# Near-attention head loads behind the last value store, reciprocals by two blocks, gates in quarters

## The chip, the cores and the metric

The kernel runs on one core of one Trainium2 chip. The metric is device time in microseconds (us) of one execution. A core has five engines with an instruction queue each: TensorE (PE, matmuls; its weight loads are PEld in the profile), VectorE (DVE), ScalarE (ACT), GpSimd (POOL) and SyncE (SP), which in this kernel issues nearly all DMA transfers. In the traces here an engine takes its instructions in the order of its queue: what waits holds up all that stands behind it.

## What is computed

A two-layer encoder on 1024 tokens of width 1024. The change lies in the second (odd) layer. Cut to that:

```python
qc, kc, vc, qm, gate = split_cols(h @ w_in_odd[o], SPLIT_ODD)
yc = neighborhood_attn(qc, kc, vc, rpb_c[o])      # 16 heads of 64
ym = memory_attn(qm, mk, mv)                      # 4 heads of 128, 256 memory tokens
y = jnp.concatenate([yc, ym], axis=-1) * jax.nn.silu(gate)
x = x + y @ w_out_odd[o]
```

`neighborhood_attn` is softmax attention on the 16 x 64 token grid in which each query sees a clamped window of 8 rows by 16 columns, with a learned bias by offset. The tokens are permuted so that for one block of 128 queries all keys lie in the block itself and its two neighbours. The kernel calls these heads the near heads.

## The kernel before, in words

**Arithmetic.** Every float32 operand of a large product is split into a high and a low part (`h`, `l`), and three products are summed. So each product first needs a copy on ACT and a subtraction on DVE or POOL, also for the transposed probabilities (`p_parts`, L527: `ph` on ACT at L117, then `pl` on DVE).

**Stages of the second layer.** After `front` (input projections, to about 1036 us), `odd` runs the memory attention (to about 1145 us) and then the near heads (`near`, about 1145 to 1393 us); `out_project` follows. While the memory attention runs, a generator `work` fills PE with what is left of the projections: the gate of one tile, the values of the last near heads (`values_of_two`, two calls `a` and `b`), and the first keys. `values_of_two` evicts each 128 tokens into a tile `vt` (ACT copy, DVE subtraction at L414) and stores it to the DRAM tensor `vd` (L415, rows `v<-vt`); there are three `vt` buffers, shared with the gate's. Behind `b` and the first keys, `work` asks for what the first near head needs: two bias tiles (`near_bias`, L1046, rows `bm<-offsets`, 320 KB each) and the values of the first pair of heads (`load_v`, rows `v<-v`, 1024 KB). The queries (`load_q`, rows `q<-qc`, two of 512 KB for a pair of heads) are asked for behind the last memory scores; those of the second pair in `near` at its third block, its values at its sixth.

**Who orders it.** The order on PE is pinned to the order of the program from `odd` on. The other queues are ordered by a scheduler that simulates the program when it is built: an instruction goes where its inputs are ready in that simulation, the earlier in the program the sooner, unless it is inside `tc.issue_after(x)`, which keeps it behind the instruction `x`. A load whose buffer is free is therefore put far ahead of its use. Each DMA also carries one of eight semaphores in turn, and is issued only when the transfer eight places before it has landed.

**The near heads.** `near` runs 16 heads of 8 query blocks, 128 steps `n`. At step `n` PE does, in this order: the transpositions of block column `n-4` (`flips`; they read the normalised probabilities `pn` of the up to three blocks that see these keys, the newest of them block `n-3`, which is transposed last), the scores of block `n`, the value products of column `n-5`, and a piece of the filling work (`fill`, 1930 columns on average). A score block goes through: DVE adds the bias and takes the negated maximum (L1079, into `st[:, 0:1]`), ACT does the exponential with its sum (L1082), DVE the reciprocal of the sum (L1083, 128x1), POOL the normalisation in place (L1084, which also halves). There are seven `pn` buffers.

**Side work.** After each score block one step of a list of jobs is issued behind that block's normalisation: the splitting of weights (L451 and L453 on POOL), and, when a pair of heads is done, `gated_steps` (L459): the output `y` of the pair is multiplied by its gate in two halves of 512 columns on DVE (L465, L467), one half a step, then combined on POOL and stored.

Of the kernel before, what the change touches and what calls it, by code (L numbers as in the profile page):

```python
# [9 lines left out]
F32 = mybir.dt.float32  # L10
F32R = mybir.dt.float32r
I32 = mybir.dt.int32
AF = mybir.ActivationFunctionType
OP = mybir.AluOpType
# [9 lines left out]
NEG = -1e30  # L24
# [7 lines left out]
O_Q, O_K, O_V, O_QM, O_G = 0, 8, 16, 24, 28  # L32
# [15 lines left out]
            c=(("P", "P"), ("P", "P"), ("P", "P"), ("yb", "yb"))),  # L48
       dict(y=(("P", "P", "q", "q", "v"), ("k", "k", "k", "k", "q", "q"), ("H",) * 6, ("H",) * 6, ("P", "P", "q", "q", "v"),
               ("k", "k", "k", "k", "q", "q"), ("H",) * 6),  # L50
            c=(("H", "H"), ("H", "H"), ("mk", "sg"), ("yb", "yb"))))
# [13 lines left out]
class Trunk:  # L65
# [317 lines left out]
    def values_of_two(self, w, vd, tag, bank, out, pieces=1, low=None):  # L383

        nc = self.nc
        n = 8 // pieces
        hs, ls = ([t[:, k:k + 2, :] for t in [self.st(tag, [128, n, 256], F32R) for _ in range(pieces)]
                   for k in range(0, n, 2)] for _ in range(2))
        for k in range(0, KT, 2):
            h, l = hs[k // 2], ls[k // 2]  # L390
            with self.ahead("w"):
                raw = self.wload(w[:, :, k * 128:k * 128 + 256].rearrange("h p n -> p h n"))
                raw = raw.rearrange("p (h k n) -> p k h n", h=2, k=2)
                h4, l4 = (t.rearrange("p k (h n) -> p k h n", h=2) for t in (h, l))
                self.copy(h4, raw)
                (low or nc.gpsimd).tensor_tensor(l4, raw, h4, op=OP.subtract)
        yield
        for b in range(0, 8, 2):
            p = self.ps(bank[b // 2 % len(bank)])
            for e in range(2):  # L400
                t = slice((b + e) * 128, (b + e) * 128 + 128)
                for kt in range(KT):
                    for i, (x, m) in enumerate(((0, hs), (0, ls), (1, hs))):
                        self.last = self.pe.matmul(p[:, 256 * e:256 * e + 256], self.h[x][kt][:, t], m[kt // 2][:, kt % 2, :],  # L404
                                                     start=e + kt + i == 0, stop=kt == KT - 1 and i == 2,
                                                     skip_group_check=True)
                    if kt % 4 == 3 and (e == 0 or kt < KT - 1):
                        yield 3072
            for e in range(2):
                o = self.st(out, [128, 2, 2, 2, 64], F32R)  # L410
                src = p[:, e * 256:(e + 1) * 256].rearrange("p (j h d) -> p j h d", j=2, h=2)
                with self.ahead("evict"):
                    self.copy(o[:, :, :, 0, :], src)
                    self.vec.tensor_tensor(o[:, :, :, 1, :], src, o[:, :, :, 0, :], op=OP.subtract)  # L414
                    nc.sync.dma_start(vd[:, :, b + e, :].rearrange("j p n -> p j n"),  # L415
                                      o.bitcast(F32).rearrange("p j h e d -> p j (h e d)"))
            yield 3072

    def gate(self, w, nt, tag="sg"):
# [39 lines left out]
    def gated_steps(self, sg, y, yd, k):  # L459

        nc = self.nc
        first, second = slice(0, 512), slice(512, T)
        dst = yd[k]
        two = lambda t: t.rearrange("p (a n) -> p a n", a=2)
        nc.vector.tensor_tensor(y[:, second], y[:, second], sg[:, second], op=OP.mult)  # L465
        yield
        nc.vector.tensor_tensor(y[:, first], y[:, first], sg[:, first], op=OP.mult)  # L467
        if k < 6:
            yield
            nc.gpsimd.tensor_tensor(sg[:, first], y[:, first], y[:, second], op=OP.subtract)  # L470
            h, l = sg.bitcast(F32R)[:, second], y.bitcast(F32R)[:, second]
            self.copy(h, y[:, second])
            nc.vector.tensor_tensor(l, y[:, second], h, op=OP.subtract)
            nc.sync.dma_start(dst[:, 0:4:2, :], two(y))
            nc.sync.dma_start(dst[:, 1:4:2, :], two(sg))
            return
        nc.sync.dma_start(dst[:, 0:2, :], two(y))
        nc.sync.dma_start(two(sg), yd[k - 6][:, 0:2, :])
        yield
        yield  # L480
        yield
        nc.gpsimd.tensor_tensor(sg[:, second], y[:, first], sg[:, second], op=OP.subtract)
        yield
        nc.gpsimd.tensor_tensor(sg[:, first], y[:, first], sg[:, first], op=OP.subtract)
        nc.sync.dma_start(dst[:, 2:4, :], two(sg))
        yield
        nc.gpsimd.tensor_tensor(y[:, second], sg[:, second], y[:, second], op=OP.subtract)
        nc.sync.dma_start(dst[:, 4, :], y[:, second])
# [554 lines left out]
    def near_bias(self, h):  # L1043

        bm = self.st("bm", [128, 5, 128])
        self.nc.sync.dma_start(bm, self.io["offsets"][h])  # L1046
        return bm

    def near(self, made, load_q, load_v, gate, yd, fill):
# [3 lines left out]

        nc = self.nc
        pts, parts, acc, pair = {}, {}, {}, {}
        first = (made["q0"], made["k0"], made["v0"])
        bms = deque(made["bm"])

        def span(b):
            return max(0, b - 1), min(8, b + 2)  # L1060

        def scores(n):
            h, b = divmod(n, 8)
            q, ks = pair[h // 2]["q"][h % 2], pair[h // 2]["k"][h % 2]
            kh, kl = ks
            lo, hi = span(b)
            w = (hi - lo) * 128
            s = self.ps("s")
            qb = q[:, b * 128:(b + 1) * 128]
            self.pe.matmul(s[:, :w], qb, kh[:, lo * 128:hi * 128], start=True, stop=False)  # L1070
            self.pe.matmul(s[:, :w], qb, kl[:, lo * 128:hi * 128], start=False, stop=True)
            pt = self.st("pn", [128, 384])
            st = self.tiny()
            k0 = (lo - b + 1) * 128
            o = pt[:, k0:k0 + w]
            bm = bms[0]
            bias = bm[:, 2:5:2, :] if b == 0 else bm[:, 0:3:2, :] if b == 7 else bm[:, 1:4, :]
            with self.ahead("exp"):
                nc.vector.tensor_tensor_reduce(o.rearrange("p (k e) -> p k e", e=128),  # L1079
                                               s[:, :w].rearrange("p (k e) -> p k e", e=128), bias,  # L1080
                                               op0=OP.add, op1=OP.min, scale=-1.0, scalar=-NEG, accum_out=st[:, 0:1])
                nc.scalar.activation(o, o, AF.Exp, bias=st[:, 0:1], scale=-1.0, accum_out=st[:, 2:3])  # L1082
                nc.vector.reciprocal(st[:, 3:4], st[:, 2:3])  # L1083
                normal = nc.gpsimd.tensor_scalar(o, o, st[:, 3:4], 0.5, op0=OP.mult, op1=OP.mult)  # L1084
            pts[n] = pt
            for jobs in (self.jobs, self.later_jobs):
                with self.tc.issue_after(normal.ins):
                    while jobs and next(jobs[0], self) is self:
                        jobs.popleft()
                    if jobs:  # L1090
                        break
# [33 lines left out]
        for n in range(128 + 5):  # L1125
# [4 lines left out]
            if n < 128:  # L1130
                j, at = divmod(n, 16)
                if at == 0:
                    if j == 0:
                        q, k, v = first
                    else:
                        q, k, v = pair.pop("q"), made[f"k{j}"], None
# [16 lines left out]
            if n >= 5:  # L1153
                values(n - 5)
                if (n - 5) % 16 == 15:
                    j = (n - 5) // 16
# [721 lines left out]
    def odd(self, w, kvd, yd, vd, mqd, qd, gd):  # L1878
# [8 lines left out]
        nc, tc = self.nc, self.tc  # L1887
# [5 lines left out]
            return sg  # L1893

        def load_q(j):
            return [self.load("q", qd[O_Q + j][i]) for i in range(2)]

        def load_v(j):
            return self.load("v", vd[j // 2][j % 2], (128, 8, 256)).rearrange("p b (h d) -> p b h d", h=2)
        with self.ahead("first"):  # L1900
            kvm = {0: self.load("k", kvd[0], (128, 4, MEM))}
            load = lambda n: self.load("q", mqd[n // 2][:, :, n % 2 * 512:n % 2 * 512 + 512].rearrange("i p n -> p i n"), (128, 2, 512))
# [1 line left out]
        made, first, begun = {}, [], []  # L1904
# [14 lines left out]
        def work():  # L1919
# [14 lines left out]
            yield from k  # L1934
            made["bm"] = [self.near_bias(i) for i in range(2)]
            made["v0"] = load_v(0)
            todo = [(O_K + 1, keys(1)), (O_K + 2, keys(2)), half(5, 0), (O_K + 3, keys(3)), half(5, 512), (O_K + 4, keys(4)),
                    (O_K + 5, keys(5)), half(6, 0), (O_K + 6, keys(6)), half(6, 512), (O_K + 7, keys(7)),
# [56 lines left out]
        for n in range(8):  # L1995
            h, g = divmod(n, 2)
            if g == 0:
                y = self.st("yb", [128, T])
# [4 lines left out]
            o = self.ps("pv")  # L2003
# [8 lines left out]
        while "open" not in made:  # L2012
            fill(1)
        self.due = 0
        self.near(made, load_q, load_v, gate, yd, lambda n: fill(STEP))
        deque(todo, 0)
        self.pe = nc.tensor
# [101 lines left out]
```

## Time and profile before

| | us |
|---|---|
| median of 3 runs | 1513.12 (1510.55 to 1514.97) |
| profiled execution, its own time | 1518.44 |
| its span (first to last instruction) | 1516.7 |
| PE busy in the span | 1480.2 (98%) |
| DVE, ACT, POOL busy | 1042.7, 840.5, 642.5 |
| memory attention and near heads, from the span's start | 1036 to 1393 |

Every duration below is of the profiled execution; 1.7 us of its time lie outside the span. A row of a timeline reads: start, duration, engine, line, operation, output<-input, shape, count, and in brackets how long the engine sat idle before and what released it. Names of tiles stand without their buffer's number. Line numbers are of the kernel before.

### The profile page before, as it was taken

What the parts mean: (1) busy time and instruction counts of PE and PEld (TensorE: products, weight loads), DVE (VectorE), ACT (ScalarE), POOL (GpSimd) and SP (SyncE); (2) the same over time, 40 slices, a digit from 0 to 9 for tenths busy, and PEclk for the clock granted to TensorE, in tenths of its full rate; (3) what the DMA queues carried; (4) which work ended last, traced back from release to release, by engine and by line L of the source; (5) the groups of instructions that cost most, each with busy time, mean ns of one, the idle gap of its engine ahead of it and who ended that gap; (6) DMA issues with size and microseconds to landing.
All of it is one profiled execution on the core that took longest, in us unless ns stands there. A gap on an engine that the chain in (4) does not pass through costs nothing.

```text
span 1516.7 us, 25292 instructions
## 1 busy us (share of the span) xinstructions
PE 1480.2 (98%) x8377; PEld 1272.6 (84%) x8377; DVE 1042.7 (69%) x2117; ACT 840.5 (55%) x1855; POOL 642.5 (42%) x766
## 2 busy tenths in 40 slices
PE   8999999999999999999999999999999999999997
PEld 8898897888888788887879877888898888888886
DVE  7686776777776667777577676654346777788754
ACT  7643664566656456655444444444346777778443
POOL 1323557746675645553450000002324555654455
PEclk9999999999999999999999999999999999999998
DMA  8956334334343524388653344567755577688833
GB/s 292 290 162 182 95 116 156 113 128 124 128 142 97 176 75 143 99 275 276 193 179 125 121 138 137 160 167 265 273 178 174 178 231 228 211 285 314 294 117 137
DMA packets 173859, 271.90 MB, mean 179 GB/s; under 512 B 15648, under 2 KB 96800, under 8 KB 172704
## 3 DMA queue, kind: packets, MB, share of 16 engines
q1 hardware_dynamic: 173296, 270.20, 55.2%
q8 instruction: 66, 1.08, 0.3%
q14 instruction: 65, 0.53, 0.1%
q10 hardware_dynamic: 432, 0.09, 0.0%
HBM read 174.28 MB, written 83.89 MB: 170 GB/s over the span
## 4 chain that ended last, share of the span: by engine, by line
PE 46%; DVE 4%; DMA 3%; issue 1%; ACT 1%; POOL 1%; SPq 0%; POOLq 0%; DVEq 0%; ACTq 0%
PE pj L62 10%; PE x L1532 6%; PE pj L1285 3%; PE pv L62 3%; PE y L1532 3%; PE sa L1285 3%; PE s L62 3%; PE s L1285 2%; PE tr L62 2%; PE tr L1285 2%; PE pv L1532 2%; PE pv L1285 2%; PE y L404 2%; PE pv L404 2%; DMA v<-vt 1%
## 5 line engine op out<-in xcount | busy, mean ns | idle before, releaser
L117 ACT ACTIVATE ph<-tr 128x512 fp32r<-128x512 f32 (+2 forms) x336 | 180.9, 540 | 123.1 <-PE tr L125 82.3
L527 DVE TENSOR_TENSOR pl<-tr,ph 128x512 fp32r<-128x512 f32 (+2 forms) x336 | 205.5, 614 | 55.2 <-ACT ph L117 54.2
L231 PE MATMUL pj<-H,wh 128*128 128x512 f32 x704 | 235.4, 414 | 0.5 <-DVE vt L302 0.2
L147 POOL TENSOR_SCALAR wh<-wraw 128x512 fp32r<-128x512 f32 x48 | 31.8, 665 | 271.3 <-PE x L1532 236.6
L117 ACT ACTIVATE wh<-wraw 128x384 fp32r<-128x384 f32 (+1 forms) x163 | 89.2, 553 | 102.4 <-PE tr L1285 13.5
L231 PE MATMUL pj<-H,wl 128*128 128x512 f32 x352 | 139.6, 397 | 0.0
L231 PEld LDWEIGHTS pj<-H,wh 128*128 128x128 f32 x704 | 120.6, 190 | 18.8 <-POOL wl L149 0.6
L62 PE MATMUL pj<-H,wh 128*128 128x512 f32 x384 | 121.4, 397 | 0.0
L125 PE MATMUL tr<-ident,P 128*128 128x128 f32 x752 | 117.5, 273 | 3.8 <-POOL P L702 1.3
L1084 POOL TENSOR_SCALAR pn<-pn,st 128x384 f32<-128x384 f32 (+1 forms) x128 | 75.2, 588 | 99.7 <-DVE st L1083 60.8
L1233 POOL TENSOR_TENSOR wl<-wraw,wh 128x384 fp32r<-128x384 f32 x56 | 64.1, 1146 | 114.4 <-ACT wh L117 80.4
L125 PEld LDWEIGHTS tr<-ident,P 128*128 128x128 f32 x752 | 89.1, 140 | 13.9 <-POOL P L702 2.6
L1005 ACT ACTIVATE P<-sa,st 128x1024 f32<-128x1024 f32 x64 | 71.6, 1118 | 45.2 <-DVE st L1004 25.4
L1082 ACT ACTIVATE pn<-pn,st 128x384 f32<-128x384 f32 (+1 forms) x128 | 75.1, 587 | 35.4 <-DVE st L1079 33.0
L1007 POOL TENSOR_SCALAR P<-P,st 128x1024 f32<-128x1024 f32 x64 | 74.3, 1164 | 33.7 <-DVE st L1006 28.9
L1004 DVE TENSOR_REDUCE st<-sa 128x1 f32<-128x1024 f32 x64 | 77.6, 1218 | 14.2 <-PE sa L1000 11.3
L62 PE MATMUL s<-k,q 128*128 128x384 f32 (+1 forms) x352 | 86.4, 341 | 0.0
L149 POOL TENSOR_TENSOR wl<-wraw,wh 128x512 fp32r<-128x512 f32 x52 | 68.2, 1313 | 27.0 <-ACT wh L117 24.1
L231 PEld LDWEIGHTS pj<-H,wl 128*128 128x128 f32 x352 | 66.4, 189 | 15.2
L62 PE MATMUL pj<-H,wl 128*128 128x512 f32 x192 | 75.8, 395 | 0.0
L821 PE MATMUL pj<-ah,H 128*128 128x256 f32 x384 | 72.5, 287 | 1.4 <-DVE H L766 1.3
L62 PEld LDWEIGHTS pj<-H,wh 128*128 128x128 f32 x384 | 66.7, 189 | 5.5
(503 smaller groups left out, 4200.6 us busy)
## 6 DMA issues: line engine op xcount, KB each, us to landing
wraw<-w_o SPq DMA_DIRECT2D x52, 256.0 KB, 3.9
y<-yb SPq DMA_DIRECT2D x24, 512.0 KB, 3.3
wraw<-s SPq DMA_DIRECT2D x64, 192.0 KB, 3.3
wraw<-w_e SPq DMA_DIRECT2D x44, 256.0 KB, 3.3
k<-k SPq DMA_DIRECT2D x42, 256.0 KB, 4.3
s<-bias SPq DMA_DIRECT2D x56, 192.0 KB, 2.0
y<-sg SPq DMA_DIRECT2D x20, 512.0 KB, 3.9
wq<-w_o SPq DMA_DIRECT2D x40, 256.0 KB, 3.6
```

What stands on the lines that cost most here:

```text
L62: return lambda *a, **k: self.tc.keep_in_program_order(getattr(self.engine, name)(*a, **k))
L117: return self.nc.scalar.activation(out, in_, AF.Copy, scale=scale)
L125: self.turned = self.fence = self.pe.transpose(o, i, self.ident)
L231: self.pe.matmul(a[:, :n], s[:, kt % UNIT, :], m, start=(kt == 0 and i == 0), stop=(kt == KT - 1 and i == 2))
L527: self.low = nc.vector.tensor_tensor(pl[:, :n], tr[:, :n], ph[:, :n], op=OP.subtract)
L821: self.last = nc.tensor.matmul(a[:, b * 256:(b + 1) * 256], x[kt][:, t], w, start=(kt + b + i == 0), stop=(kt == KT - 1 and i == 2), skip_ ...
L1004: nc.vector.tensor_reduce(st[:, 0:1], s, axis=AX.X, op=OP.max, negate=True)
L1007: self.normal = nc.gpsimd.tensor_scalar(pt, pt, st[:, 2:3], 0.5, op0=OP.mult, op1=OP.mult)
L1082: nc.scalar.activation(o, o, AF.Exp, bias=st[:, 0:1], scale=-1.0, accum_out=st[:, 2:3])
L1084: normal = nc.gpsimd.tensor_scalar(o, o, st[:, 3:4], 0.5, op0=OP.mult, op1=OP.mult)
L1285: last = nc.tensor.matmul(bank, s[:, k, :], y[3 * u + k][m][:, cols], start=start and u + k + e == 0, stop=u == 1 and k + e == 4, skip_gro ...
L1532: self.last = nc.tensor.matmul(bank, ws[s][:, k, :], b[k][m], start=start and k + i == 0, stop=k == UNIT - 1 and i == 2, skip_group_check= ...
```

## The change

Three edits. First, the last store of values is remembered (`self.stored`), and `near_bias`, `load_q` and `load_v` are issued behind it. Second, the statistics of two successive blocks share one `st` tile; the reciprocal is taken once for both, when the second block's sum is there, and then both are normalised one after the other. `self.normal`, behind which the jobs are issued, is then the last normalisation that there is: for a block with an even number that of the pair before. Third, `gated_steps` multiplies in four quarters of 256 columns, one a step.

```diff
@@ values_of_two
-                    nc.sync.dma_start(vd[:, :, b + e, :].rearrange("j p n -> p j n"),
+                    self.stored = nc.sync.dma_start(vd[:, :, b + e, :].rearrange("j p n -> p j n"),
...
@@ gated_steps
-        nc.vector.tensor_tensor(y[:, second], y[:, second], sg[:, second], op=OP.mult)
-        yield
-        nc.vector.tensor_tensor(y[:, first], y[:, first], sg[:, first], op=OP.mult)
+        for i, c in enumerate(slice(p, p + 256) for p in (512, 768, 0, 256)):
+            nc.vector.tensor_tensor(y[:, c], y[:, c], sg[:, c], op=OP.mult)
+            if i < 3:
+                yield
@@ near_bias
-        self.nc.sync.dma_start(bm, self.io["offsets"][h])
+        with self.tc.issue_after(self.stored.ins):
+            self.nc.sync.dma_start(bm, self.io["offsets"][h])
@@ near, scores(n)
-            st = self.tiny()
+            if not begun:
+                begun.append(self.tiny())
+            st, e = begun[0], n % 2
...
-                nc.scalar.activation(o, o, AF.Exp, bias=st[:, 0:1], scale=-1.0, accum_out=st[:, 2:3])
-                nc.vector.reciprocal(st[:, 3:4], st[:, 2:3])
-                normal = nc.gpsimd.tensor_scalar(o, o, st[:, 3:4], 0.5, op0=OP.mult, op1=OP.mult)
+                nc.scalar.activation(o, o, AF.Exp, bias=st[:, e:e + 1], scale=-1.0, accum_out=st[:, 2 + e:3 + e])
+                begun.append(o)
+                if e:
+                    nc.vector.reciprocal(st[:, 4:6], st[:, 2:4])
+                    for i, p in enumerate(begun[1:]):
+                        self.normal = nc.gpsimd.tensor_scalar(p, p, st[:, 4 + i:5 + i], 0.5, op0=OP.mult, op1=OP.mult)
+                    begun.clear()
             pts[n] = pt
             for jobs in (self.jobs, self.later_jobs):
-                with self.tc.issue_after(normal.ins):
+                with self.tc.issue_after(self.normal.ins):
@@ odd
         def load_q(j):
-            return [self.load("q", qd[O_Q + j][i]) for i in range(2)]
+            with tc.issue_after(self.stored.ins):
+                return [self.load("q", qd[O_Q + j][i]) for i in range(2)]
         def load_v(j):
-            return self.load("v", vd[j // 2][j % 2], (128, 8, 256)).rearrange("p b (h d) -> p b h d", h=2)
+            with tc.issue_after(self.stored.ins):
+                v = self.load("v", vd[j // 2][j % 2], (128, 8, 256))
+            return v.rearrange("p b (h d) -> p b h d", h=2)
```

The build shows what the queues become. In the changed kernel the lines after L415 are higher by a few (L985 is L986, L1079 is L1084, L1083 is L1090, L527 is L528).

On SP, in the second half of the memory attention, before. `v_12663` and `v_12843` are the values of the first two pairs of heads, `y_0` and `y_1` the stores of gated memory heads, the rows with `vt` the stores of values.

```order
L506 DMA y_0_83<-sg_12002 128x2x512
L985 DMA v_12663<-v_103 128x2048
L505 DMA y_0_83<-yb_11728 128x2x512
L985 DMA v_12843<-v_103 128x2048
L415 DMA v_105<-vt_12065 128x2x256
L415 DMA v_105<-vt_12069 128x2x256
L1892 DMA sg_12296<-g_9281 128x1024
L415 DMA v_106<-vt_12177 128x2x256
L985 DMA q_12613<-qc_9288 128x1024
L415 DMA v_106<-vt_12181 128x2x256
```

And in the changed kernel, from the last two stores of values on (the names of the loads are the same):

```order
L415 DMA v_106<-vt_12471 128x2x256
L415 DMA v_106<-vt_12475 128x2x256
L986 DMA q_12613<-qc_9288 128x1024
L986 DMA q_12615<-qc_9288 128x1024
L1048 DMA bm_12659<-offsets 128x640
L1048 DMA bm_12661<-offsets 128x640
L986 DMA v_12663<-v_103 128x2048
L986 DMA q_12780<-qc_9289 128x1024
L986 DMA v_12837<-v_103 128x2048
L986 DMA q_12782<-qc_9289 128x1024
L507 DMA y_2_85<-sg_12552 128x2x512
```

Before, ten stores of values stood behind the first `v` load; now all eight first loads of the near heads stand together behind the last store.

On DVE, where the third pair of heads runs and the second pair's `y` is gated, before. `pn_13641` and `pn_13666` are the probabilities of two successive blocks, 34 and 35; L467 multiplies a half of `y`; `pl` is the low part that PE's value products wait for.

```order
L1079 ISA pn_13641,st_13642<-s_13638,bm_13342 128x384
L1079 ISA st_13642 128x1
L467 TENSOR_TENSOR yb_13291<-yb_13291,mk_13317 128x512
L527 TENSOR_TENSOR pl_13635<-tr_13630,ph_13634 128x384
L1079 ISA pn_13666,st_13667<-s_13663,bm_13342 128x384
```

The same blocks in the changed kernel:

```order
L1084 ISA pn_13609,st_13610<-s_13606,bm_13318 128x384
L1084 ISA st_13610 128x1
L466 TENSOR_TENSOR yb_13269<-yb_13269,mk_13293 128x256 x2
L528 TENSOR_TENSOR pl_13603<-tr_13598,ph_13602 128x384
L1084 ISA pn_13632,st_13610<-s_13629,bm_13318 128x384
```

The half has become two quarters in direct succession, at the same place ahead of `pl`. Of the 32 quarters 26 stand so, in 13 couples; six stand apart.

On DVE in the twelfth head, blocks 90, 91 and 92 before (`pn_15209`, `pn_15231`, `pn_15253`, with the reciprocals of their `st` tiles):

```order
L1079 ISA pn_15209,st_15210<-s_15206,bm_14897 128x384
L1079 ISA st_15210 128x1
L527 TENSOR_TENSOR pl_15203<-tr_15198,ph_15202 128x384
L1079 ISA pn_15231,st_15232<-s_15228,bm_14897 128x384
L1079 ISA st_15232 128x1
L1083 RECIPROCAL st_15210<-st_15210 128x1
L527 TENSOR_TENSOR pl_15225<-tr_15221,ph_15224 128x256
L1083 RECIPROCAL st_15232<-st_15232 128x1
L1079 ISA pn_15253,st_15254<-s_15250,bm_14897 128x384
```

The same three blocks in the changed kernel (`pn_15128`, `pn_15148`, `pn_15170`; blocks 90 and 91 share `st_15129`):

```order
L1084 ISA pn_15128,st_15129<-s_15125,bm_14825 128x384
L1084 ISA st_15129 128x1
L528 TENSOR_TENSOR pl_15122<-tr_15117,ph_15121 128x384
L1132 TENSOR_TENSOR yb_14986<-pv_14987,bt_15099 64x512
L1084 ISA pn_15148,st_15129<-s_15145,bm_14825 128x384
L1084 ISA st_15129 128x1
L528 TENSOR_TENSOR pl_15142<-tr_15138,ph_15141 128x256
L1084 ISA pn_15170,st_15171<-s_15167,bm_14825 128x384
L1084 ISA st_15171 128x1
L1090 RECIPROCAL st_15129<-st_15129 128x2
```

The reciprocal that blocks 90 and 91 need has moved behind the bias step of block 92. Of the 64 pairs this holds for seven: the first (blocks 0 and 1), and those that begin with blocks 12, 44, 52, 90, 116 and 122. For the other 57 the reciprocal stands ahead of the next pair.

More of the change, by code (lines that the diff above doesn't have):

```diff
@@ L414, in values_of_two @@
                     self.vec.tensor_tensor(o[:, :, :, 1, :], src, o[:, :, :, 0, :], op=OP.subtract)
-                    nc.sync.dma_start(vd[:, :, b + e, :].rearrange("j p n -> p j n"),
-                                      o.bitcast(F32).rearrange("p j h e d -> p j (h e d)"))
+                    self.stored = nc.sync.dma_start(vd[:, :, b + e, :].rearrange("j p n -> p j n"),
+                                                    o.bitcast(F32).rearrange("p j h e d -> p j (h e d)"))
             yield 3072
@@ L1055, in near @@
         pts, parts, acc, pair = {}, {}, {}, {}
+        begun = []
         first = (made["q0"], made["k0"], made["v0"])
@@ L1080, in scores @@
                                                s[:, :w].rearrange("p (k e) -> p k e", e=128), bias,
[L1081 to L1084, printed above, removed]
+                                               op0=OP.add, op1=OP.min, scale=-1.0, scalar=-NEG, accum_out=st[:, e:e + 1])
+                nc.scalar.activation(o, o, AF.Exp, bias=st[:, e:e + 1], scale=-1.0, accum_out=st[:, 2 + e:3 + e])
[5 more added lines that the diff above has]
+                    begun.clear()
             pts[n] = pt
             for jobs in (self.jobs, self.later_jobs):
-                with self.tc.issue_after(normal.ins):
+                with self.tc.issue_after(self.normal.ins):
                     while jobs and next(jobs[0], self) is self:
```

## The prediction

> **What bounds the kernel now.** I read the page first, for the busy shares, then who waited for whom on PE between 1080 and 1396 us, where all three edits act, then the timelines around the waits.
>
> ```profile
> span 1516.7 us, 25292 instructions
> ...
> PE 1480.2 (98%) x8377; PEld 1272.6 (84%) x8377; DVE 1042.7 (69%) x2117; ACT 840.5 (55%) x1855; POOL 642.5 (42%) x766
> ```
>
> ```profile
> PE pv L62 <- DVE pl L527: 3.7, 7, 1.1
> PE pv L62 <- ACT ph L117: 2.9, 1, 2.9
> PE tr L62 <- POOL pn L1084: 0.2, 1, 0.2
> ```
>
> PE works 98% of the span. Here it stood still for 6.8 us: once for 2.9 us behind a `ph` of ACT, seven times behind a `pl` of DVE, once for a normalisation on POOL. The edits do not touch PE's own work, so beside its clock only these waits can be won, and only new ones lost. The long one:
>
> ```profile
> 1081.17 0.42 SPq L985 DMA_DIRECT2D v<-v  x1
> ...
> 1082.60 0.56 SPq L985 DMA_DIRECT2D v<-v  x1
> 1083.25 2.62 SPq L415 DMA_DIRECT2D v<-vt  x2
> ```
>
> ```profile
> 1083.25 12.62 DMA v<-vt
> ...
> 1095.95 0.38 ACT vt L117
> ```
>
> Behind two 1024 KB loads of values, a store `v<-vt` took 12.6 us on the chain of waits, until 1095.87. ACT needed its `vt` buffer, and the next `ph` stood behind that copy. In windows (length, then PE busy; the clock is the figure ahead of the last two):
>
> ```profile
> 1095.00:1098.00 3.00, 0.21 (x1) 0.21 (x2) 0.82 (x3) 1.78 (x6) 0.46 (x2) 1.00 0.65 255
> ...
> 1099.00:1102.00 3.00, 3.00 (x16) 3.00 (x15) 0.69 (x1) 0.60 (x1) 0.00 (x0) 0.50 0.38 89
> 1102.00:1103.00 1.00, 1.00 (x10) 1.00 (x9) 0.12 (x1) 0.39 (x1) 0.00 (x0) 0.89 0.73 299
> 1103.00:1145.00 42.00, 42.00 (x263) 37.34 (x262) 19.15 (x35) 19.07 (x49) 8.15 (x14) 1.00 0.59 176
> ```
>
> After the stop PE's clock is 0.50 for 3 us and 0.89 for one more: with the first tenth or so lost before 1099, some 1.7 us. The stop costs 2.9 + 1.7 = 4.6 us.
>
> **Part 1, the loads: -4.6 us.** With both `v` loads behind the last store, the store at 1083 has only the gated tiles ahead of it. The lateness to be cut is 1097.79 (where PE went on) less 1094.93, 2.9 us of 12.6; without the 2.1 MB of `v` loads it has some 5 us less to wait, by the rate below. What moved is eight loads:
>
> ```profile
> v<-v SPq DMA_DIRECT2D x8, 1024.0 KB, 6.0
> q<-qc SPq DMA_DIRECT2D x16, 512.0 KB, 4.5
> ...
> bm<-offsets SPq DMA_DIRECT2D x16, 320.0 KB, 5.9
> ```
>
> ```profile
> 1091.00:1093.00 2.00, 2.00 (x19) 2.00 (x18) 0.69 (x1) 0.00 (x0) 0.09 (x1) 1.00 1.02 393
> ```
>
> ```profile
> 1120.21 1.02 SPq L415 DMA_DIRECT2D v<-vt  x2
> ```
>
> ```profile
> 1144.48 0.40 PE L62 MATMUL s<-k,q 128*128 128x256 f32 x2
> ```
>
> Together 2 x 1024 + 4 x 512 + 2 x 320 = 4736 KB, 4.85 MB. At the 393 GB/s that the loaded window moved this is 12 us. The last stores went out from 1120.2 to 1121.2 before (now near 1116); the first near scores were at 1144.5 (now near 1140). So 24 us of memory attention cover the loads, beside 176 GB/s that was there already. I cost them at nothing; without the cover each microsecond of lateness is one of PE's. On SP they also stand ahead of a gate's stores and the first keys' copies; the last of them waits for PE's last memory scores, as it did before.
>
> **Part 2, the pairs: +2.5 us, and +0.5 us at the start.** It saves 64 reciprocals of these on DVE:
>
> ```profile
> L1083 DVE RECIPROCAL st<-st 128x1 f32<-128x1 f32 x128 | 20.2, 158 | 18.3 <-ACT pn L1082 17.5
> ...
> L414 DVE TENSOR_TENSOR vt<-pj,vt 128x256 fp32r<-128x256 f32 x16 | 6.7, 421 | 10.9 <-ACT vt L117 10.6
> ...
> L467 DVE TENSOR_TENSOR yb<-yb,mk 128x512 f32<-128x512 f32 x4 | 2.9, 737 | 0.0
> ```
>
> That is 64 x 0.158 = 10 us of an engine that is not the bound: nothing by itself. The price is that a pair's first block is normalised one step later, while its transposition stays at step n+3. What counts is the time from the second block's scores to that transposition. A common case, blocks 74 and 75 (the scores of 75, a weight split on POOL, the bias step of 75, its reciprocal and normalisation, the transposition that first reads 74):
>
> ```profile
> 1287.45 0.59 PE L62 MATMUL s<-k,q 128*128 128x384 f32 x2
> ...
> 1288.10 1.29 POOL L453 TENSOR_TENSOR wl<-wraw,wh 128x512 fp32r<-128x512 f32 x1
> ...
> 1288.19 0.56 DVE L1079 CUSTOM_DVE_ANT_0 pn<-s,bm 128x384 f32<-128x384 f32 x1 [0.81 <-POOL pn L1084]
> ...
> 1289.53 0.16 DVE L1083 RECIPROCAL st<-st 128x1 f32<-128x1 f32 x1 [0.44 <-ACT pn L1082]
> ...
> 1289.87 0.59 POOL L1084 TENSOR_SCALAR pn<-pn,st 128x384 f32<-128x384 f32 x1 [0.48 <-PE pv L62]
> ...
> 1290.43 0.38 PE L62 MATMUL tr<-ident,pn 128*128 128x128 f32 x2
> ```
>
> The scores end at 1288.04; the chain is through at 1290.46, 2.42 us later, and block 74 would then be normalised in the place of 75. PE wants it at 1290.43: 0.03 us late. The pairs that open a head have over 1.1 us to spare, but for the very first. Of the 48 others I compared each pair's four rows in this way: 24 come within 0.3 us of their transposition. How far late is too late the one such wait before shows:
>
> ```profile
> 1151.32 0.59 POOL L1084 TENSOR_SCALAR pn<-pn,st 128x384 f32<-128x384 f32 x1
> ...
> 1151.35 0.38 PE L62 MATMUL tr<-ident,pn 128*128 128x128 f32 x2
> ...
> 1151.96 0.33 PE L62 MATMUL tr<-ident,pn 128*128 128x128 f32 x1 [0.23 <-POOL pn L1084]
> 1151.96 0.36 PEld L62 LDWEIGHTS s<-k,q 128*128 128x128 f32 x2
> 1152.05 0.59 PE L62 MATMUL s<-k,q 128*128 128x384 f32 x2
> ```
>
> Normalised 0.56 us (1151.91) after its group began, the block held the scores up to 1152.05, 0.70 us behind the group instead of the usual 0.25: 0.45 us. So 0.1 us is free, as the newest block is transposed last, and pairs like 74 cost nothing. Dear are the pairs whose reciprocal stands behind the next block's bias step. For blocks 90 and 91:
>
> ```profile
> 1320.09 0.56 DVE L1079 CUSTOM_DVE_ANT_0 pn<-s,bm 128x384 f32<-128x384 f32 x1 [0.37 <-PE pv L62]
> ...
> 1320.70 0.49 PE L62 MATMUL tr<-ident,pn 128*128 128x128 f32 x3
> ```
>
> The step of 92 ends at 1320.65; with reciprocal 0.16, hand-over 0.17 and normalisation 0.59 it is 1321.57, 0.87 late, less 0.1: 0.8 us. Worked the same way the pairs of 12, 116 and 122 give 0.6, 0.5 and 0.1, those of 44 and 52 nothing; two ordinary pairs (38, 50) that DVE serves late give 0.3 and 0.2. Sum 2.5 us. The first pair:
>
> ```profile
> 1149.24 0.16 DVE L1083 RECIPROCAL st<-st 128x1 f32<-128x1 f32 x1
> ...
> 1149.50 0.59 POOL L1084 TENSOR_SCALAR pn<-pn,st 128x384 f32<-128x384 f32 x1 [0.55 <-DVE st L1083]
> ...
> 1150.14 0.14 PEld L62 LDWEIGHTS tr<-ident,pn 128*128 128x128 f32 x1 [0.29 <-POOL pn L1084]
> ```
>
> PE already waited 0.29 us there for block 1. Its reciprocal can come no earlier as one of 128x2; a normalisation of block 0 (128x256, some 0.5 us, two thirds of the 0.59 and a fixed part) now goes ahead of it: +0.5 us.
>
> The bounds: 0 if DVE, relieved, hands on a little earlier everywhere, and 8.2 us if the 24 close pairs come 0.4 us later than I take them (the sum with 0.3 us less room instead of 0.1 more).
>
> **Part 3, the quarters: +0.5 us.** Two quarters cost 2 x 0.42 = 0.84 us by the 128x256 row above, a half 0.74. In the order 13 of 16 halves merely become two adjoining quarters at the same place before `pl`, so the waits they cause stay:
>
> ```profile
> 1210.30 0.45 PE L62 MATMUL pv<-pl,v 128*128 128x384 f32 x1 [0.79 <-DVE pl L527]
> ```
>
> 0.1 us more in each of some five such waits is 0.5 us. Bounds: -2.5, if all of the six waits inside the stage went (3.7 less the 1.1 at its end), and +1.3 (13 x 0.1).
>
> **Sum.** -4.6 + 2.5 + 0.5 + 0.5 = -1.1 us. The profiled execution took 1518.4 us, so 1517.3; it stands 5.3 us above the median of the runs shown, 1513.1, on which scale I forecast **1512 us**.
>
> **Rivals.** (a) *The pairs cost nothing, or the quarters do come apart on the chip*: -4.6 and up to -2.5, so 1506 to 1508.5, say 1507. For it: DVE loses 10 us of work and 64 stops behind ACT (17.5 us of idle in the row above). Against: in close pairs the bias step already starts as soon as PE's scores are there (1288.19, 0.15 us behind them). (b) *Slower: close margins turn into waits.* The place is the transposition of a pair's first block; it decides once the 2.42 us chain grows by some 0.3 us in the 24 close pairs, for example because POOL has two normalisations at once behind a 1.3 us weight split. Price 8.2 or more: -4.6 + 8.2 + 1 = +4.6, with a second block caught now and then 1519. (c) *The stop costs only itself*: if the half clock came of this execution's chance, the loads win 2.9 us and the sum is +0.6: 1514. [...]
>
> **How the numbers follow.** Forecast (1510 to 1515): 0.38; (c), 1514: 0.14; (a): 0.25; (b): 0.23. What a measurement can tell from no change is 0.3%, 4.5 us, so faster is below 1508.6 and slower above 1517.7: faster 0.25, same 0.52, slower 0.23. The range from 1506.5 to 1519 leaves out the far ends of (a) and (b).
>
> **What would show it.** Right: no wait of PE for `ph` near 1095 and clock 1.00 from 1080 to 1145; waits of `tr` for `pn` of 2 to 4 us in all, longest around the named pairs; `pl` waits of about 4 us still. Wrong: a store of values still late; `tr` waits of 8 us, which is (b), or under 1, which is (a); a wait of the first near scores for a load.

## The result and the profile after

The changed kernel took **1516.79 us** (median of 18 executions, 1512.61 to 1521.52), the kernel before 1511.97 (18 executions, 1507.60 to 1517.36): ratio 1.0032, 95% interval 1.0022 to 1.0042. It is slower by 4.8 us, where I had forecast 1.1 us faster. The profiled execution of the change took 1515.52 us, less than the 1518.44 of the one before: that one stood above each of the 18 executions timed here, and this matters below. The ratios below leave out two executions that were far slower than all others, one of the kernel with the quarters alone (2415.57 us) and one of the kernel before (4597.43).

The page after, its first lines:

```profile
span 1513.7 us, 25246 instructions
...
PE 1478.0 (98%) x8377; PEld 1269.0 (84%) x8377; DVE 1036.2 (68%) x2069; ACT 841.2 (56%) x1855; POOL 641.8 (42%) x766
```

DVE has lost 48 instructions and 6.5 us of work; PE, busy for 98% of the span, still bounds. Who PE waited for between 1080 and 1396 us after (total, times, longest):

```profile
PE pv L62 <- DVE pl L528: 4.6, 7, 1.2
PE tr L62 <- POOL pn L1092: 3.9, 7, 0.9
```

The wait for `ph` of 2.9 us is gone, 0.9 us more goes to `pl`, and 3.7 us more to normalisations. In windows (length, busy times, then the clock), where the stop and the halved clock had been:

```profile
1080.00:1098.00 18.00, 18.00 (x145) 17.56 (x144) 7.70 (x14) 7.78 (x21) 3.14 (x5) 1.00 0.43 144
1098.00:1103.00 5.00, 5.00 (x42) 4.82 (x41) 2.59 (x7) 2.53 (x9) 1.88 (x5) 1.00 0.70 254
```

PE is busy throughout at full clock. The near stage runs, after, between these scores, its first and its last block's:

```profile
1134.62 0.40 PE L62 MATMUL s<-k,q 128*128 128x256 f32 x2
...
1382.19 0.48 PE L62 MATMUL s<-k,q 128*128 128x256 f32 x2
```

That is 247.57 us. Before it was 1144.48 to 1385.05, 240.57: the stage has grown by 7.0 us. I number the 128 blocks' steps by their scores, from 0, and compare, before and after, the time from one step's scores to the next; growth "at 4" is that of the time between the scores of blocks 3 and 4. The largest growth is at 4 (+1.26), 127 (+1.14), 87 and 103 (+1.03 each), 119 (+0.84) and 53 (+0.76). At step 87 the timeline after shows, for DVE (the gate's two quarters, then the low part), POOL (two subtractions for another gate) and PE:

```profile
1299.63 2.04 DVE L466 TENSOR_TENSOR yb<-yb,sg 128x256 f32<-128x256 f32 x2
1301.60 0.54 DVE L528 TENSOR_TENSOR pl<-tr,ph 128x384 fp32r<-128x384 f32 x1
```

```profile
1298.66 1.30 POOL L483 TENSOR_TENSOR mk<-yb,mk 128x512 f32<-128x512 f32 x1
1299.91 1.48 POOL L485 TENSOR_TENSOR mk<-yb,mk 128x512 f32<-128x512 f32 x1
```

```profile
1302.19 0.44 PE L62 MATMUL pv<-pl,v 128*128 128x384 f32 x1 [0.76 <-DVE pl L528]
```

Two quarters that I had priced at 0.84 us took 2.04, `pl` came late, and PE waited 0.76 us. Before, at the same step, DVE's half and the low part behind it, and POOL's normalisation:

```profile
1307.28 0.92 DVE L465 TENSOR_TENSOR yb<-yb,sg 128x512 f32<-128x512 f32 x1
...
1308.12 0.54 DVE L527 TENSOR_TENSOR pl<-tr,ph 128x384 fp32r<-128x384 f32 x1
```

```profile
1307.07 0.59 POOL L1084 TENSOR_SCALAR pn<-pn,st 128x384 f32<-128x384 f32 x1
```

### The profile page after: what moved, and what is told of

It is laid out like the page before. It is cut to its first block, busy times and chain, and to the rows that moved or that the text cites. A ratio compares the mean times of both kernels' runs of the same rounds, so it can differ in the third digit from the quotient of the medians.

```text
span 1513.7 us, 25246 instructions
## 1 busy us (share of the span) xinstructions
PE 1478.0 (98%) x8377; PEld 1269.0 (84%) x8377; DVE 1036.2 (68%) x2069; ACT 841.2 (56%) x1855; POOL 641.8 (42%) x766
## 4 chain that ended last, share of the span: by engine, by line
PE 43%; DVE 5%; DMA 4%; issue 2%; POOL 1%; ACT 1%; SPq 0%; POOLq 0%; DVEq 0%; ACTq 0%
PE pj L62 9%; PE x L1541 6%; PE pj L1294 3%; PE y L1541 3%; PE sa L1294 3%; PE pv L62 3%; PE s L62 3%; PE tr L62 2%; PE tr L1294 2%; PE pv L1541 2%; PE s L1294 2%; PE pv L1294 2%; PE pv L404 2%; PE y L404 1%; DMA y<-yb 1%
## 5 line engine op out<-in xcount | busy, mean ns | idle before, releaser
L528 DVE TENSOR_TENSOR pl<-tr,ph 128x512 fp32r<-128x512 f32 (+2 forms) x336 | 205.6, 615 | 52.0 <-ACT ph L117 50.9
L231 PEld LDWEIGHTS pj<-H,wh 128*128 128x128 f32 x704 | 120.3, 190 | 18.4 <-POOL wl L149 0.6
L1084 DVE CUSTOM_DVE_ANT_0 pn<-s,bm 128x384 f32<-128x384 f32 x96 | 53.1, 553 | 28.1 <-PE s L62 20.7
```

What stands on the lines that cost most here:

```text
L231: self.pe.matmul(a[:, :n], s[:, kt % UNIT, :], m, start=(kt == 0 and i == 0), stop=(kt == KT - 1 and i == 2))
L528: self.low = nc.vector.tensor_tensor(pl[:, :n], tr[:, :n], ph[:, :n], op=OP.subtract)
```

## The experiments

Two questions. First, the loads: near +7.0 with a gain of 4.6 in front of it would be +2.4, and +4.8 was measured. Theory A: the stop comes in every execution of before, and the near stage costs 9.4 in the timed ones. Theory B: a stop of 2.9 us belongs to that one execution. Second, what in the near stage costs: the pairs, as the forecast had it, or the quarters.

Measured (near stage: growth of the time from first to last near scores in the one profiled execution; us by the ratio on 1512). Two more variants of the pairs, of which only the profiled execution was timed, and the loops that compute nothing of the model follow in the text:

| kernel | near, us | ratio (95%) | us |
|---|---|---|---|
| before, second profile | +0.45 | | |
| loads | +0.8 | 0.9993 (0.9977 to 1.0010) | -1.1 |
| pairs | +1.45 | 1.0007 (0.9991 to 1.0022) | +1.1 |
| quarters | +4.2 | 1.0035 (1.0014 to 1.0056) | +5.3 |
| loads and pairs | +2.65 | 1.0003 (0.9987 to 1.0018) | +0.5 |
| late half split | +2.9 | 1.0027 (1.0014 to 1.0041) | +4.1 |
| early half split | -0.4 | 1.0000 (0.9985 to 1.0014) | 0.0 |
| halves, later steps | +1.65 | 1.0002 (0.9988 to 1.0017) | +0.3 |
| loads, early half split | +0.7 | 0.9993 (0.9978 to 1.0007) | -1.1 |
| the change | +7.0 | 1.0032 (1.0022 to 1.0042) | +4.8 |

The second profile of the unchanged kernel says how far the near column is to be trusted: 0.45 us.

**The kernel before, a second profile** (no edit).

> The kernel before, unchanged, profiled a second time. The first profiled execution stood 6.5 us above the median of the timed ones (1518.4 against 1512.0), and the loads' term rests on one stop that it shows. Theory A: the stop belongs to the program's order of transfers and comes in every execution; then this trace again shows PE waiting 2 to 4 us for `ph` near 1095 us and some 4 us of halved clock behind it, and from the first product of the odd blocks to the first near scores again 108 +- 1 us. Theory B: the stop needs a store that happens to be slow; then this trace shows no such wait or one under 1 us, that stretch takes 103 to 105 us, and the whole is near 1512.

Its waits of PE from 1080 us on, and from its chain of waits the store and the eviction that it held up:

```profile
PE pv L62 <- DVE pl L527: 3.7, 7, 1.1
PE pv L62 <- ACT ph L117: 0.4, 1, 0.4
PE tr L62 <- POOL pn L1084: 0.2, 1, 0.2
```

```profile
1083.44 10.24 DMA v<-vt
...
1093.76 0.38 ACT vt L117
```

The near stage's waits recur to a tenth; the stop does not: the same store took 10.24 us instead of 12.62, and PE waited 0.4 us, with a like one of 0.4 at 1060. The stretch ahead of the near scores took 105.25 us instead of 108.36, just above theory B's 103 to 105, and the execution 1515.14, 3 above its 1512. The other kernels here that keep the old order of loads waited for `ph` 0.5 to 1.5 us between 1040 and 1396 (0.8, 0.9, 1.5, 0.5, 1.2, 1.3, 1.1). That fits theory B: 2.9 us is the largest of nine traces. Near a wait of 1.5 us the clock stayed at 1.00, here of the kernel with the late half split:

```profile
1090.00:1095.00 5.00, 3.46 (x25) 2.76 (x24) 1.28 (x3) 1.79 (x6) 0.94 (x2) 1.00 0.90 348
1095.00:1100.00 5.00, 5.00 (x41) 4.87 (x40) 1.74 (x4) 1.96 (x4) 0.00 (x0) 1.00 0.59 194
```

In each of the eight traces beside the first the clock is 1.00 from 1040 to 1395 us: most executions probably had no half clock to win either.

**Loads alone.** The edit is the change's first part: `self.stored`, and

```diff
-        self.nc.sync.dma_start(bm, self.io["offsets"][h])
+        with self.tc.issue_after(self.stored.ins):
+            self.nc.sync.dma_start(bm, self.io["offsets"][h])
```

with the same around the loads in `load_q` and `load_v`.

> Only part 1: the first loads of the near heads behind the last store of values. Theory A (the stop of 2.9 us and the half clock behind it are in every execution): -4.6 us, 1507.4 on a median of 1512, ratio 0.997, and the near stage unchanged within 1 us. The near edits would then cost 9.4 us in the timed executions, to make +4.8 in all. Theory B (the stop belongs mostly to the profiled execution of before): 0 to -2.5 us, ratio 0.9983 to 1.000, and the near edits cost what the traces show, 7.1.

-1.1 us, between -3.5 and +1.5: theory B's range, and not to be told from nothing; A's 4.6 lies outside. The traces say where it comes from. The stretch from the first product of the odd blocks to the first near scores takes 104.75 to 105.72 us in the eight other traces with the old order of loads, and 103.38 to 103.42 in the four that have the loads behind the last store: about 1.8 us less, and no wait for `ph`; the stores of values that follow each other from 1075 to 1102 landed in 2.1 to 4.9 us. But 0.8 us of it is lost at step 4, where a first transposition now waits for POOL; that leaves 1.0, as timed. This loss too comes of the loads. DVE multiplies the last memory head by its gate ahead of the first bias step; now, and then before:

```profile
1134.58 1.23 DVE L499 TENSOR_TENSOR yb<-yb,sg 128x1024 f32<-128x1024 f32 x1 [3.02 <-DMA sg<-g]
```

```profile
1144.62 1.23 DVE L499 TENSOR_TENSOR yb<-yb,sg 128x1024 f32<-128x1024 f32 x1 [2.03 <-ACT yb L117]
```

The load of that gate now stands in SP's queue behind copies of the first keys. It was issued 5.8 us ahead of the first near scores instead of 9.3, and the product began 1.13 us behind these scores instead of 0.14.

**Pairs alone.** The edit is the change's part in `near`:

```diff
-                nc.vector.reciprocal(st[:, 3:4], st[:, 2:3])
-                normal = nc.gpsimd.tensor_scalar(o, o, st[:, 3:4], 0.5, op0=OP.mult, op1=OP.mult)
+                if e:
+                    nc.vector.reciprocal(st[:, 4:6], st[:, 2:4])
...
```

> Only part 2: reciprocals for two blocks at once. From the traces of before and of the change: +2.1 us at the start of the near stage and 3.6 in the waits of transpositions, +5.7, ratio 1.0038. The forecast's own sum for this part was +3.0 (1.0020). Rival: the whole surplus over the forecast comes from the quarters or from the parts acting together; then at most +3.0. If theory A of the loads holds, some 8 us (1.0053).

+1.1 us (-1.4 to +3.3), so not 5.7; the forecast's 3.0 lies inside the interval. The waits of PE in its trace:

```profile
PE pv L62 <- DVE pl L527: 2.5, 4, 1.1
PE tr L62 <- POOL pn L1090: 1.6, 4, 0.8
```

Steps 4, 5, 15, 34, 41, 53, 119 and 125 cost 3.45 us together, but 39, 47, 55 and 71 come 1.5 us sooner: the waits for `pl` fell from 3.7 to 2.5.

**Quarters alone.** The edit:

```diff
-        nc.vector.tensor_tensor(y[:, second], y[:, second], sg[:, second], op=OP.mult)
-        yield
-        nc.vector.tensor_tensor(y[:, first], y[:, first], sg[:, first], op=OP.mult)
+        for i, c in enumerate(slice(p, p + 256) for p in (512, 768, 0, 256)):
+            nc.vector.tensor_tensor(y[:, c], y[:, c], sg[:, c], op=OP.mult)
+            if i < 3:
+                yield
```

> Only part 3: gates multiplied in quarters. The change's trace shows the waits of pv for pl some 1.4 us longer in sum than before: +1.4 us, ratio 1.0009. The forecast's term was +0.5 (1.0003). Rival: that growth comes of the pairs, which move DVE's work beside the quarters; then the quarters alone give 0 +- 0.5. If the quarters came apart on the chip, -2.5.

+5.3 us (+2.1 to +8.5): the quarters alone carry the loss, and none of the three expectations had it. PE's waits in its trace:

```profile
PE pv L62 <- DVE pl L528: 7.4, 11, 1.2
```

The two quarters of step 87, each by itself, and POOL beside them:

```profile
1297.36 0.65 DVE L466 TENSOR_TENSOR yb<-yb,sg 128x256 f32<-128x256 f32 x1
```

```profile
1297.93 1.50 DVE L466 TENSOR_TENSOR yb<-yb,sg 128x256 f32<-128x256 f32 x1
```

```profile
1297.15 0.59 POOL L1085 TENSOR_SCALAR pn<-pn,st 128x384 f32<-128x384 f32 x1
1297.71 1.44 POOL L485 TENSOR_TENSOR mk<-yb,mk 128x512 f32<-128x512 f32 x1
```

The first quarter began while a normalisation ran and ended 0.27 us behind it. POOL's next operation began then, and the second quarter ended 0.28 us behind that one. This fits what the expectations below call theory P: the two engines take turns, instruction by instruction, and a split gives POOL a turn in the middle.

**The change without its quarters** (the two edits above together).

> The change without its quarters: loads and pairs only. If the quarters carry the loss (alone they took 1518.5, +6.5 on the median of before, at 1.0035), this stands near before: the sum of -1.5 (loads alone) and +1.7 (pairs alone) is 1512, ratio 1.000 +- 0.0015. If the pairs cost what I read from the change's trace (5.7), it is 1516 to 1517, 1.003, and the quarters' loss does not add to it.

1.0003: at before's time. Taking out the quarters alone takes the 4.8 us away.

**The late half split.** Which half pays? DVE multiplies columns 512 to 1023 second. Against before:

```diff
+        for i, (a, b) in enumerate(((512, 768), (768, 1024), (0, 512))):
+            nc.vector.tensor_tensor(y[:, a:b], y[:, a:b], sg[:, a:b], op=OP.mult)
+            if i < 2:
+                yield
```

> Halves as before but for columns 512 to 1023, the half that DVE multiplies second in its order: two quarters there. In the trace of the quarters alone three of these adjoining quarters took 1.5 us instead of 0.42, each while POOL ran a subtraction or a weight split. Theory P (POOL's next long operation comes in between two quarters of two SBUF operands and DVE waits for its end; a half left no such opening): this half carries it, +2.8 us near (steps 23, 87 and 103: 0.6, 1.1, 1.1), ratio 1.0018, and the second quarter again 1.4 to 1.5 us where POOL runs beside it. Theory S (what costs is that all that follows the gate comes two steps later): only half of the later steps are here, about +2, spread over waits elsewhere, and quarters of 0.42. Theory D (each quarter's own 0.1 us): +0.4.

+4.1 us (+2.1 to +6.2), near +2.9, with +1.13 at step 87 and +1.11 at 103; at 23 nothing, there POOL's next operation came later here. The gates' products on `yb` and `mk` (ns: least, median, most):

```profile
L466 DVE TENSOR_TENSOR yb<-yb,mk x12: 410/648/1504, 1203.5 to 1402.6; 128x256 f32<-128x256 f32 x8, 128x512 f32<-128x512 f32 x4
```

**The early half split**: the same with `((512, 1024), (0, 256), (256, 512))`.

> The other half split alone (columns 0 to 511, which DVE multiplies first): two quarters there, the other half whole. Before, POOL was idle beside these halves but for a normalisation. Theory P: no quarter above 0.8 us and no new wait from a stalled quarter; only what moves where the two quarters stand a step apart (step 53 +0.9, steps 47 and 55 -0.5 and -0.7): 0 +- 1 us, ratio 1.000. Theory S: as much as the other half, +2. Theory D: +0.4.

0.0 us (-2.3 to +2.1). The same row has no long instruction; its 0.92 is a half:

```profile
L466 DVE TENSOR_TENSOR yb<-yb,mk x12: 404/422/917, 1199.8 to 1395.1; 128x256 f32<-128x256 f32 x8, 128x512 f32<-128x512 f32 x4
```

Theory D falls: the two splits are equal in count, and only one of them costs.

**Halves with the quarters' later steps.** Two more steps between the halves:

```diff
         yield
+        yield
+        yield
         nc.vector.tensor_tensor(y[:, first], y[:, first], sg[:, first], op=OP.mult)
```

> Halves as before, but with the two further steps between them that the quarters bring, so that all that follows (POOL's subtraction, the low part, the stores) is issued when the quarters issue it. Theory P: only the wait of the gated tile for its store's buffer at step 92 (+0.7) and step 110 (+0.4): +0.5 to +1.2 us, ratio 1.0005. Theory S: the whole loss of the quarters, +4 to +6, ratio 1.003 to 1.004.

+0.3 us (-1.8 to +2.6); the trace has +1.65, as much as step 92 alone, where P had +0.7; S's 4 to 6 is out. At step 87 POOL stands as in the quarters' trace, a gate's subtraction right behind the normalisation:

```profile
1300.69 0.92 DVE L465 TENSOR_TENSOR yb<-yb,sg 128x512 f32<-128x512 f32 x1
```

```profile
1300.48 0.59 POOL L1086 TENSOR_SCALAR pn<-pn,st 128x384 f32<-128x384 f32 x1
1301.03 1.72 POOL L486 TENSOR_TENSOR mk<-yb,mk 128x512 f32<-128x512 f32 x1
```

Here the half is done at 1301.61 and it is POOL's operation that stretches, from 1.3 to 1.72 us. POOL had time, DVE had not. So the loss needs two things at once: an operation of POOL that has come up behind the normalisation (the later steps bring it) and a cut through the half at that place.

**The turns by themselves.** None of the model is computed; DVE and POOL run short loops side by side:

```diff
+        for vec in (half, quarters, low, scale):
+            for pool in (None, sub, norm):
...
+                for _ in range(8):
+                    vec()
```

> None of the model is computed: DVE runs eight halves (128x512, two SBUF operands), eight pairs of quarters, eight differences with one operand in PSUM, and eight products by a constant (one SBUF operand), each first with POOL idle, then beside twelve subtractions on POOL (128x512, two operands, 1.29 us alone), then beside twelve normalisations (128x384, 0.59 alone). Theory P (the two engines exclude each other for the whole of an instruction, and the place changes hands at each end): with POOL idle 0.55 to 0.67 a half and 0.3 to 0.42 a quarter; beside the subtractions every DVE instruction waits for one of them, so a half takes 1.8 to 2.0 us and each quarter 1.5 to 1.6, two quarters 3.1, so 1.2 us more for the same product; beside the normalisations a half 1.1 and two quarters 1.7. The differences from PSUM stay at their 0.55 to 0.7 whatever POOL does. If instead the two share bandwidth, two quarters beside POOL take about what a half takes there, plus 0.1 to 0.2.

In windows (length; DVE busy and its instructions, POOL busy and its), in order: halves with POOL idle, beside subtractions, beside normalisations; quarters the same; differences with one operand in PSUM, with POOL idle and beside subtractions; products by a constant beside subtractions:

```profile
8.88:14.66 5.78, 5.54 (x8) 0.00 (x0) 1.00 0.00 0
16.14:27.78 11.64, 11.43 (x7) 11.09 (x8) 1.00 0.00 0
35.75:42.64 6.89, 6.68 (x7) 6.24 (x8) 1.00 0.00 0
48.01:53.47 5.46, 5.46 (x16) 0.00 (x0) 1.00 0.00 2
54.34:71.17 16.83, 16.83 (x13) 15.97 (x12) 1.00 0.00 0
73.97:80.88 6.91, 6.91 (x15) 6.26 (x8) 1.00 0.00 0
86.16:91.93 5.77, 5.53 (x8) 0.00 (x0) 1.00 0.00 0
92.69:98.46 5.77, 5.53 (x8) 5.34 (x5) 1.00 0.00 1
124.78:134.55 9.77, 9.56 (x7) 9.22 (x8) 1.00 0.00 0
```

Four of the windows beside POOL, those of the halves, of the quarters beside normalisations and of the products by a constant, begin behind the first half, pair of quarters or product, which ran before POOL had begun to hold DVE up. Alone, a half takes 5.78 / 8 = 0.72 us and two quarters 5.46 / 8 = 0.68: splitting costs nothing of itself. Beside subtractions a half takes 11.64 / 7 = 1.66, with one subtraction for each, and a quarter 16.83 / 12 = 1.40, again one for each: two quarters 2.8, so 1.1 us more. That is the +1.1 of steps 87 and 103. One operand in PSUM frees DVE of it: 0.72 in both rows. So the turns of theory P are there, and shared bandwidth, by which two quarters would have taken 0.1 to 0.2 us more than a half, is out.

Two sizes of theory P were missed. Beside subtractions a half takes less than the 1.8 to 2.0 expected and a quarter less than 1.5 to 1.6: a half (0.72) and a subtraction (1.3) alone make 2.0 us, so in 1.66 some 0.4 us of the two go on side by side, and that they exclude each other for the whole of an instruction is not shown. And beside normalisations two quarters take 6.91 / 7 = 0.99, as much as a half (6.89 / 7 = 0.98), with one normalisation for both, where 1.7 was expected. There POOL did not get its turn between quarters; why is open.

**Loads and the early half split**, the parts that were free or better.

> A version that keeps what the runs showed to be free or better: the loads behind the last store, quarters only in the half that DVE multiplies first (columns 0 to 511), no pairs. Sum of the two alone: -1.5 and 0 us, 1511, ratio 0.999 (interval 0.9975 to 1.001); near stage within 1 us of before. If the parts spoil one another, as the late half did, 1.002.

0.9993 (0.9978 to 1.0007): clearly below the change, and not to be told from before or from the loads alone.

**Pairs with the first block's reciprocal put back.**

```diff
                 begun.append(o)
+                if not e:
+                    nc.vector.reciprocal(st[:, 4:5], st[:, 2:3])
                 if e:
```

> Pairs alone, but with the reciprocal of a pair's first block put back on DVE behind its exponential (its result is not used: the one for two blocks overwrites it). In the trace of the pairs alone the waits of pv for pl fell from 3.7 to 2.5 us, at steps 39, 47, 55 and 71 by 0.2, 0.5, 0.5 and 0.3. If that came from the 64 reciprocals taken off DVE, these four come back (1.5 us) and the near stage is 2.5 to 3.5 us longer than before's, which is the forecast's own 3.0 that left this gain out. If it came from where POOL normalises, they stay away: +1.45 as in the pairs alone.

Steps 39, 47, 55 and 71 kept their gain (-0.22, -0.51, -0.43, -0.22), so there it is not the 64 reciprocals. The near stage grew by 2.4, the further 0.95 at other places, step 109 (+0.32) and many small ones; so much the reciprocals may be worth there, by this one trace. For step 55 the two timelines show what it is instead. DVE's half in the pairs alone, then before:

```profile
1239.67 0.69 DVE L465 TENSOR_TENSOR yb<-yb,sg 128x512 f32<-128x512 f32 x1
```

```profile
1246.12 0.91 DVE L465 TENSOR_TENSOR yb<-yb,sg 128x512 f32<-128x512 f32 x1
```

Before, a normalisation of POOL ran from 1245.90 to 1246.49, and the half that began beside it took 0.91 us. With pairs two run together, from 1237.67 to 1238.82, and the half that begins behind them takes 0.69.

**Pairs from block 4 on.**

```diff
+                if lone:
+                    nc.vector.reciprocal(st[:, 4:5], st[:, 2 + e:3 + e])
...
```

with `lone` for blocks 0 to 3.

> Pairs alone, but only from block 4 on; blocks 0 to 3 are normalised singly as before. If the +0.46 and +0.58 us at steps 4 and 5 of the pairs alone are the first pairs' late normalisation, both go, and the near stage is 0.4 us longer than before's instead of 1.45. If they stay, they come from elsewhere at the stage's start.

Steps 4 and 5 fell back to before's time, the rest stayed, near +0.5: the 1.04 us were the first pairs' late normalisation.

## Why the prediction was wrong, point by point

- **Part 3, the quarters (+0.5, bounds -2.5 to +1.3): the step that failed.** "In the order 13 of 16 halves merely become two adjoining quarters at the same place" held; that each couple costs 0.1 us more did not. I took the 0.42 of a 128x256 row whose one operand comes from PSUM; both of a quarter's come from SBUF, and in the loops such a quarter took 1.40 us beside a subtraction of POOL instead of 0.34. In three couples of the quarters' trace the second quarter waited out an operation of POOL and took 0.83, 1.50 and 1.51 us. Measured: +5.3 alone, of it +4.1 in the late half. The upper bound lacked the case in which something comes in between; the halves of 0.67 and 0.92 us in the trace of before were the hint, and their list beside POOL's would have shown that each 0.92 begins inside a normalisation.
- **Part 1, the loads (-4.6): the mechanism right, the size wrong.** The `ph` wait is gone, the near loads come in time, the clock is 1.00. But 2.9 + 1.7 us was one execution's; the timed gain is 1.1 (-3.5 to +1.5). The traces bear it out: the other eight waited 0.5 to 1.5 us for `ph`, the stretch ahead of the near scores became some 1.8 shorter, and 0.8 was lost again at step 4. That loss was not in the sum: I had the loads stand ahead of other transfers on SP at no cost, and a gate's load came late. The scale was the warning: I noted that the profiled execution stood 5.3 us over the median and still took its stop at full size. Rival (c), which spared the half clock, was nearer, and still too high.
- **Part 2, the pairs (+3.0): the costs about right in sum, partly by luck, and a gain left out.** Measured +1.1 (-1.4 to +3.3), near +1.45. The costs are 3.45 in that trace, at five of the named pairs (12, 38, 50, 116 and 122 for steps 15, 41, 53, 119, 125), at step 34, which no list had, and at the start, which cost 1.0 and not 0.5. Pair 122 cost 0.75 instead of 0.1 and pair 90 nothing instead of 0.8: these errors cancel by luck. Left out was 1.5 us of gain at four waits for `pl`. In the whole change, where POOL is also later by the quarters, `tr` waits came to 3.9 us, inside my 2 to 4, and include 0.9 at step 127 that no list had. There POOL has two subtractions of a gate and a weight split ahead of the last normalisations; the subtractions begin 4.2 us ahead of the last scores, and without the quarters 7.8. Neither the quarters nor the pairs alone lose time at 127.
- **Rival (b)** had the right sign, by another mechanism: the 24 close pairs did not turn into waits. None of my rivals had the quarters as the loss. That 1516.79 lies between 1506.5 and 1519 is luck: the room above was rival (b)'s.
- Measured alone, the parts are -1.1, +1.1 and +5.3 where the forecast had -4.6, +3.0 and +0.5; together they make +5.3, and +4.8 was measured. In the trace the quarters' share of the change is 7.0 - 2.65 = 4.35 us; steps 87 and 103 carry 2.06. The other 2.3 lies at 20, 53, 93, 111, 119 and 127, less gains elsewhere; I did not follow each to its cause.

## What to carry to other kernels

Before an elementwise operation on DVE with both operands in SBUF is cut in two, look at what POOL has queued at that place: each cut can be a place where POOL's next operation comes first. Here that cost 1.1 us beside subtractions of 1.3 us (two quarters 2.8, a half 1.66); beside normalisations it cost nothing (0.99 for two quarters, 0.98 for a half). A stop in one profiled execution is worth its measured size only if it recurs; when that execution lies well above the median of the timed ones, profile it again before pricing the stop. When an operation's duration has two values in the trace (0.67 and 0.92), find what stands beside the longer one before using either.

## What the runs showed of the hardware

- In the loops DVE's products with both operands in SBUF and POOL's subtractions alternated one for one: a 128x512 product took 1.66 us instead of 0.72, a 128x256 product 1.40 instead of 0.34, each beside a subtraction of 1.3 us. A product by a constant with one SBUF operand was held too: 9.77 / 7 = 1.40 us beside subtractions, 3.65 / 8 = 0.46 with POOL idle. A difference with one operand in PSUM was not: 0.72 in both cases.
- Beside normalisations of 128x384 two quarters went through in a row (0.99 us for both, a half 0.98). The alternation was not strict there.
- PE's clock was halved after a stop of 2.86 us in the first profile of before (0.50 for 3 us) and stayed at 1.00 around one of 1.5 us in that of the late half split; each is one case.
